# Recurrence pairs moved between attention's pairs in the first pass, memory pairs moved to its end, and the second query block of a head requested with the first

## The chip, the cores and the metric

The kernel runs on one core of a Trainium2 chip. Five engines work side by side: TensorE (PE in the profile, its weight loads PEld), VectorE (DVE), ScalarE (ACT), GpSimd (POOL) and SyncE (SP), which here issues nearly all DMAs. The metric is the device time of one execution in microseconds; the median of three runs of the kernel before is 1471.98 us (1469.74 to 1475.14).

## What is computed

One decoder layer for one sequence of 2048 tokens of width 1024, in float32. The input is normalised, projected once, and the projection's columns feed three groups of heads; their outputs are joined, projected again, normalised and added to the input.

```
hn = rms_norm(x, g_pre);  proj = hn @ w_in                      # 2048 x 4096
rg_x, rg_g, da_q, da_k, da_v, da_g, xa_q, xa_g = split(proj)    # 512 columns each
# recurrence group ("rg")
xc = causal_depthwise_conv(rg_x, conv_w, conv_b)                # width 4
r, i = sigmoid(xc @ w_rg_a + b_a), sigmoid(xc @ w_rg_x + b_x)   # per 64-wide head
a = exp(-8 r softplus(-lru_lambda));  u = sqrt(1 - a*a) * (i * xc)
h[t] = a[t] h[t-1] + u[t];  y_rg = h * silu(rg_g)
# differential attention, 4 heads, causal ("qk", "v", "g")
p = softmax(q1 k1^T / 8) - lam * softmax(q2 k2^T / 8);  o = p @ v
y_da = rms_norm(o, g_subln) * (1 - lambda_init) * silu(da_g)
# memory cross attention, 4 heads, 256 memory tokens ("xa")
y_xa = softmax(xa_q km^T / sqrt(128)) @ vm * silu(xa_g)         # km, vm from rms_norm(mem) @ w_mem_kv
out = x + rms_norm(concat(y_rg, y_da, y_xa) @ w_out, g_post)
```

## The kernel before, in words

Every float32 product is made of three products of a high and a low part (`mm3`), so a projection unit of 128 columns by 512 tokens is 24 matmuls. The sequence is cut into four chunks of 512 tokens. `project` is called twice: the first pass takes chunks 0 and 1, the second chunks 2 and 3. Each pass walks through 16 positions; at each it takes one pair of column blocks from `PAIRS` (lines 41 to 48), in four units (u = 0 to 3: two chunks, two blocks). The list has, by index: 0 and 1, queries and keys of heads 0 and 1 ("qk"); 2 and 3, values and gates of those heads ("v", "g"); 4 and 5, queries and keys of heads 2 and 3; 6 and 7, their values and gates; 8 to 11, the memory group ("xa"); 12 to 15, the recurrence group ("rg"). The first pass takes them in this order (`range(16)`, line 944); the second has an order of its own, `ORDER_B` (line 50): 0, 12, 2, 13, 1, 14, 3, 15, 4, 8, 6, 9, 7, 10, 11, 5.

**Weights.** In the first pass `w_conv` splits each piece of weights into high and low part, on ScalarE and GpSimd, and loads the piece three further on (`w_load`); the split pieces are stored to the DRAM tiles `WD[pair][piece]` (line 341) and read back from there in the second pass (line 334). `wsrc` (line 316) lists the pieces in the order of use.

**The order of TensorE's work** is written out by the program. Side work lives in generators (`spawn`), and `pump` lets those go on whose planned time has come, after every three matmuls of the projection. A planned clock (`now`) counts matmuls alone. `drain` lets the side work go on without the projection until a condition holds. The order on the other engines is made by the framework's scheduler, from priorities (`tc.high_priority`) and its own estimates.

- *Attention* is two streams, started at position 2 by `start_attention` (line 909): `s_stream` (line 698) makes scores and softmax for jobs of 256 queries, with a planned distance of 3.08 us between score steps in the first pass, and `t_stream` (line 773) transposes the probabilities and multiplies them with the values. The first 16 jobs are the first 1024 queries of heads 0 to 3; `s_stream` may hold 12 buffers of probabilities. `t_stream` does not begin a head before that head's gate pair is stored (line 778), and the keys and values of head 3 are not loaded before the second pass (line 660).
- *Queries.* `q2_load(i)` (line 702) asks for query block i, two blocks a job, with two DMAs on SP's queue from the DRAM tile `QD`. Block 2j is asked for while the job before it runs (or, for the very first, as soon as its pair is stored, line 709); block 2j+1 when block 2j is taken up (line 721).
- *Memory group.* `ev_xa` (line 518) evicts a unit; `xa_steps` (line 532) makes scores, softmax and output. At its first unit (line 857) the pass drains until no recurrence work is alive, drops the recurrence weights (`rgh`) and loads the memory's keys and values (`load_km`, four DMAs of 512 KB).
- *Recurrence group.* `ev_rg` (line 583) evicts a unit and, for the first block, makes the convolution on VectorE (L597, L600, cast L603) and the low part of its result on GpSimd (L604); it drains memory work for odd chunks. `rg_gates` (line 614) waits until no memory work is alive, loads and splits the recurrence weights if they are not there (`rg_weights`, line 575), makes the two gates (matmul into `rgo`), and then the scan (L637) and the product with the gate (L640).
- *Next chunks.* At position 13, `next_x` (line 919) drains until the first 12 jobs (heads 0 to 2) are done, and starts the norms of chunks 2 and 3 (`norm_steps`, scaling at L291); at position 15 the transposes of chunk 2 begin.

Of the kernel before, what the change touches and what calls it, by code (L numbers as in the profile page):

```python
# [46 lines left out]
    + [("rg", b, (b, 4 + b)) for b in range(4)]  # L47
)

ORDER_B = (0, 12, 2, 13, 1, 14, 3, 15, 4, 8, 6, 9, 7, 10, 11, 5)  # L50
MEM_PAIRS = [(0, 1), (2, 3), (4, 5), (6, 7)]

# [5 lines left out]
def hybrid_layer(  # L58
# [30 lines left out]
    def f4(name, shape=(128, 1024), dt=F32, pool=p4):  # L89
        return pool.tile(list(shape), dt, tag="f4", name=name)  # L90

    def f2(name, shape=(128, 516), dt=F32, pool=p2):
        return pool.tile(list(shape), dt, tag="f2", name=name)
# [7 lines left out]
    def ps_s(name, shape=(128, 512)):  # L101
        return psS.tile(list(shape), F32, tag="S", name=name)
# [7 lines left out]
    def asf(ap):  # L110
        return ap.bitcast(F32)
# [7 lines left out]
    WD = [[dr.tile([128, 1024], F32, name=f"WD{p}{i}") for i in range(4)] for p in range(16)]  # L119
# [77 lines left out]
    def mm(o, w, xx, start, stop):  # L197
        nc.tensor.matmul(o, w, xx, start=start, stop=stop)  # L198
        now[0] += max(o.free_size(), 256) / 2400.0
# [8 lines left out]
    def store(fn, delay):  # L208

        def go():  # L210
            fn()
            return
            yield
        spawn(go(), delay)
# [22 lines left out]
    def split_weight(raw, hi, lo, eng=nc.gpsimd):  # L237
        nc.scalar.copy(hi, raw)  # L238
        eng.tensor_sub(lo, raw, asf(hi))  # L239
# [73 lines left out]
    def pair_pieces(ps):  # L313
        return [w_in[4 * p + i] for p in ps for i in range(4)]

    wsrc = (pair_pieces(range(2)) + [w_mem[i] for i in range(16)] + pair_pieces(range(2, 16))
            + pair_pieces(ORDER_B))
    MEM0, WB0 = 8, 80
    wraw, wcv = {}, {}

    def w_load(*ids):
        for i in ids:
            if i < WB0:
                wraw[i] = praw.tile([128, 512], F32, tag="raw", name="wraw")
                nc.sync.dma_start(wraw[i], wsrc[i])

    def w_conv(*ids, eng=nc.gpsimd, pool=pw):
        for i in ids:
            if i < len(wsrc) and i not in wcv:
                w = wcv[i] = f4("wp", (128, 2, 2, 256), F32R, pool)  # L330
                if i >= WB0:

                    q = ORDER_B[(i - WB0) // 4]
                    nc.sync.dma_start(asf(w).rearrange("p a b c -> p (a b c)"), WD[q][i % 4])
                    continue
                split_weight(wraw.pop(i), w[:, 0].rearrange("p a b -> p (a b)"),
                             w[:, 1].rearrange("p a b -> p (a b)"), eng)
                w_load(i + 3)
                if not MEM0 <= i < MEM0 + 16:
                    q = i if i < MEM0 else i - 16  # L340
                    store(lambda w=w, q=q: nc.sync.dma_start(
                        WD[q // 4][q % 4], asf(w).rearrange("p a b c -> p (a b c)")), 4.0)


    def load_rows(src, n, name):
# [18 lines left out]

    hnT = {}
    memT = []
    state = {}
    ready = set()
    stored = set()
    setup()  # L370
# [5 lines left out]
    for i in range(4):  # L376
        nc.sync.dma_start(xb[:, i].rearrange("p a b -> p (a b)"), x[CH + i * 128:CH + (i + 1) * 128, :])
    mrows = load_rows(mem, 2, "memx")
    w_conv(0)
    for row in xr0:  # L380
        norm_row(row)
    w_conv(1, 2, eng=nc.vector)

    def woven(c, rows):
# [266 lines left out]
    def has(kind, idx, part):  # L651
        return (kind, idx, part) in stored
# [35 lines left out]
    def load_q2(h, qb):  # L688
        t = f2("q2", (128, 2, 2, 128), F32R)
        cs = slice((qb % 4) * 128, (qb % 4) * 128 + 128)  # L690
        for ab in range(2):
            nc.sync.dma_start(asf(t[:, ab]), QD[h][qb // 4][:, ab:ab + 2, :, cs].rearrange("c l r t -> (l r) c t"))
        return t

    def pace(i):
        return PACE[0 if "b" not in state else 2 if state["kind"] == "out" else 1][i]

    def s_stream(jobs):

        q2s = {}  # L700

        def q2_load(i):
            if i < 2 * len(jobs) and i not in q2s:
                h, pr = jobs[i // 2]
                if has("qk", h, pr // 4):
                    q2s[i] = load_q2(h, 2 * pr + i % 2)
        due = now[0]
        for ij, (h, pr) in enumerate(jobs):
            while 2 * ij not in q2s:
                q2_load(2 * ij)  # L710
                yield 0.5
            while kready.get((h, pr // 4), 1e9) > now[0]:
                yield 0.5
            due = max(due, now[0] - 3.0)
            ks = kt[h, pr // 4]
            P = []
            for b in range(2):
                qb = 2 * pr + b
                q2_load(2 * ij + b)
                q2 = q2s.pop(2 * ij + b)  # L720
                q2_load(2 * ij + b + 1)
                kend = (qb + 1) * 128
                nk = (kend + 511) // 512
                nm = tiny.tile([128, 2, nk], F32, tag="nm", name="nm")
                l = tiny.tile([128, 2, nk], F32, tag="l", name="l")
                e = {}
                for kc in range(nk):
                    w = min(512, kend - 512 * kc)
                    while room["e"] < 2:
                        yield 0.4  # L730
                    room["e"] -= 2
                    for c in range(2):
                        e[kc, c] = f2("e", (128, 512), pool=pe)
                        s = ps_s("s")
                        for ab in range(2):
                            mm(s[:, 0:w], q2[:, ab, c, :], ks[kc][:, c, 0:w], ab == 0, ab == 1)
                        with tc.high_priority(offset=PRS):
                            if kc == nk - 1:
                                nc.vector.tensor_add(s[:, w - 128:w], s[:, w - 128:w], cmask)
                            nc.vector.tensor_reduce(out=nm[:, c, kc:kc + 1], in_=s[:, 0:w], op=ALU.max, axis=AX.X,  # L740
                                                    negate=True)
                            nc.scalar.activation(e[kc, c][:, 0:w], s[:, 0:w], AF.Exp, bias=nm[:, c, kc:kc + 1],  # L742
                                                 accum_out=l[:, c, kc:kc + 1])
                        due += pace(0)
                        yield max(S_GAP, due - now[0])
                with tc.high_priority(offset=PRN):
                    f = tiny.tile([128, 2, nk], F32, tag="f", name="f")
                    if nk == 1:
                        nc.vector.reciprocal(f, l)
                        nc.vector.tensor_mul(f[:, 1, :], f[:, 1, :], nlam)  # L750
                    else:
                        m = tiny.tile([128, 2, 1], F32, tag="m", name="m")
                        r = tiny.tile([128, 2, 1], F32, tag="r", name="r")
                        nc.vector.tensor_reduce(out=m, in_=nm, op=ALU.min, axis=AX.X)
                        nc.vector.tensor_sub(f, m.to_broadcast([128, 2, nk]), nm)
                        nc.scalar.activation(f, f, AF.Exp)
                        nc.vector.tensor_mul(l, l, f)
                        nc.vector.tensor_reduce(out=r, in_=l, op=ALU.add, axis=AX.X)
                        nc.vector.reciprocal(r, r)
                        nc.vector.tensor_mul(r[:, 1, :], r[:, 1, :], nlam)  # L760
                        nc.vector.tensor_mul(f, f, r.to_broadcast([128, 2, nk]))  # L761
                    for kc in range(nk):
                        w = min(512, kend - 512 * kc)
                        e1, e2 = (e[kc, c][:, 0:w] for c in range(2))
                        nc.gpsimd.tensor_scalar(e2, e2, f[:, 1, kc:kc + 1], 1.0, op0=ALU.mult, op1=ALU.mult)  # L765
                        nc.vector.scalar_tensor_tensor(e1, e1, f[:, 0, kc:kc + 1], e2, op0=ALU.mult, op1=ALU.add)  # L766
                P.append([e[kc, 0] for kc in range(nk)])
                room["e"] += nk
            probs[h, pr] = now[0] + pace(1), P
            if pr == 7:  # L770
                room["kv"] += 1
# [167 lines left out]
    def start_b():  # L939
# [1 line left out]
        room["kv"] += 1  # L941
        spawn(prep_next(3))

    project((0, 1), 0, range(16), {
        (2, 0): start_attention,
        (13, 0): next_x,
        (15, 2): lambda: spawn(prep_next(2)),
# [30 lines left out]

    project((2, 3), 80, ORDER_B, {(0, 0): start_b, (15, 2): last_pair})

# [117 lines left out]
```

## Time and profile before

| | us |
|---|---|
| median of three runs | 1471.98 |
| the three runs | 1469.74, 1471.98, 1475.14 |
| the profiled execution, as timed | 1467.53 |
| its span, from the first to the last instruction | 1465.7 |
| TensorE busy | 1412.3 |
| VectorE busy | 898.3 |
| ScalarE busy | 775.9 |
| GpSimd busy | 477.3 |

The share of a busy engine is taken over the whole span. Matmul durations overlap, so TensorE's busy time is the union of them. By the eviction instructions, the first pass's positions 4 to 11 run from 153 to 425 us of the span (memory pairs from 275 on), its positions 12 to 15 (recurrence) from 425 to 548, the second pass's positions 0 to 7 from 548 to about 787, its memory pairs between 800 and 1080; from 1080 on the output projection runs. The clock in the tables is the mean granted to TensorE, 1.00 being full speed.

### The profile page before, as it was taken

To read this page: it belongs to the slowest core of one execution; us is meant where nothing else is said; L and a number is where in the kernel's file an instruction comes from. 1 tells how busy PE (TensorE), PEld (TensorE's weight loads), DVE (VectorE), ACT (ScalarE), POOL (GpSimd) and SP (SyncE) were. 2 spreads that over 40 slices of the span, in tenths; PEclk is the share of its full clock that TensorE was granted. 3 is DMA by queue.
4 is the path that set the end of the run, shared out by engine and by line. 5 is a ranking of instruction groups with operands and counts; after the bars stand their busy time and mean duration, and the time that the engine had idled before them with its cause. 6 is when DMAs were issued, how large, how long until landed. Compare 5 with 4: busy or idle time off the path is not lost.

```text
span 1465.7 us, 21854 instructions
## 1 busy us (share of the span) xinstructions
PE 1412.3 (96%) x7568; PEld 1199.2 (82%) x7568; DVE 898.3 (61%) x1872; ACT 775.9 (53%) x1900; POOL 477.3 (33%) x568
## 2 busy tenths in 40 slices
PE   5999999999999899999999999999999999999997
PEld 3798889888887678888887898888877888888886
DVE  6531555676644876746547666757678777767222
ACT  6343544666547784745555545555566545554221
POOL 2031333344435632412213222212255333334221
PEclk9999999999999999999999999999999999999999
DMA  8689787745433348356324554232475334322231
GB/s 298 180 263 338 230 240 237 247 143 181 166 119 110 134 163 247 121 173 196 114 97 118 165 177 168 86 113 70 143 251 169 101 135 150 102 76 94 87 122 72
DMA packets 147870, 234.37 MB, mean 160 GB/s; under 512 B 12464, under 2 KB 82224, under 8 KB 147760
## 3 DMA queue, kind: packets, MB, share of 16 engines
q1 hardware_dynamic: 147616, 232.98, 48.8%
q8 instruction: 59, 0.97, 0.3%
q14 instruction: 51, 0.42, 0.1%
q10 hardware_dynamic: 144, 0.01, 0.0%
HBM read 142.76 MB, written 90.18 MB: 159 GB/s over the span
## 4 chain that ended last, share of the span: by engine, by line
PE 73%; DVE 9%; ACT 7%; DMA 4%; POOL 3%; issue 3%; SPq 1%; DVEq 0%; POOLq 0%; ACTq 0%
PE ip L198 36%; PE po L198 16%; PE s L198 7%; PE o L198 6%; PE pt L202 3%; PE xas L198 2%; DVE e L766 1%; DVE nm L740 1%; PE xao L198 1%; DMA q<-QD 1%; DVE xc L600 1%; PE rgo L198 1%; ACT e L742 1%; PE xat L202 1%; POOL e L765 1%
## 5 line engine op out<-in xcount | busy, mean ns | idle before, releaser
L198 PE MATMUL ip<-hnT,wp 128*128 128x512 f32 x2688 | 680.5, 397 | 6.9 <-DVE rgg L610 2.6
L198 PEld LDWEIGHTS ip<-hnT,wp 128*128 128x128 f32 x2688 | 496.0, 190 | 109.8 <-DVE hnT L307 4.5
L742 ACT ACTIVATE e<-s,nm 128x512 f32<-128x512 f32 (+3 forms) x320 | 200.1, 626 | 254.7 <-DVE nm L740 235.8
L740 DVE TENSOR_REDUCE nm<-s 128x1 f32<-128x512 f32 (+3 forms) x320 | 193.4, 605 | 37.4 <-PE s L198 33.1
L198 PE MATMUL po<-wout,yg 128*128 128x512 f32 x768 | 193.4, 393 | 5.0 <-POOL wout L239 2.4
L765 POOL TENSOR_SCALAR e<-e,f 128x512 f32<-128x512 f32 (+3 forms) x160 | 121.3, 773 | 235.5 <-DVE f L761 161.6
L198 PE MATMUL s<-kv,q 128*128 128x512 f32 (+3 forms) x640 | 182.9, 367 | 3.9 <-DMA q<-QD 2.4
L198 PEld LDWEIGHTS po<-wout,yg 128*128 128x128 f32 x768 | 141.1, 188 | 35.4 <-POOL wout L239 4.2
L766 DVE SCALAR_TENSOR_TENSOR e<-e,f 128x512 f32<-128x512 f32 (+3 forms) x160 | 138.0, 887 | 29.9 <-POOL e L765 29.7
L807 DVE TENSOR_TENSOR pthl<-pt,pthl 128x512 fp32r<-128x512 f32 (+1 forms) x144 | 94.5, 656 | 68.0 <-ACT pthl L806 67.5
L198 PE MATMUL o<-pthl,kv 128*128 128x256 f32 (+1 forms) x864 | 134.3, 290 | 1.0 <-DVE pthl L807 0.9
L198 PEld LDWEIGHTS s<-kv,q 128*128 128x128 f32 x640 | 114.5, 189 | 25.1 <-DMA q<-QD 3.0
L239 POOL TENSOR_TENSOR wp<-wraw,wp 128x512 fp32r<-128x512 f32 x67 | 91.1, 1368 | 127.1 <-ACT wp L238 110.8
L198 PEld LDWEIGHTS o<-pthl,kv 128*128 128x128 f32 x864 | 114.1, 189 | 4.5 <-DVE pthl L807 1.8
L806 ACT CAST pthl<-pt 128x512 fp32r<-128x512 f32 (+1 forms) x144 | 80.7, 561 | 55.2 <-PE pt L202 54.5
L239 POOL TENSOR_TENSOR yg<-yraw,yg 128x512 fp32r<-128x512 f32 x48 | 64.2, 1341 | 132.8 <-ACT yg L238 122.4
L198 PE MATMUL ip<-wp,hnT 128*128 128x256 f32 x768 | 99.7, 284 | 1.3 <-POOL wp L239 0.8
L198 PEld LDWEIGHTS ip<-wp,hnT 128*128 128x128 f32 x768 | 95.8, 191 | 3.0 <-POOL wp L239 1.0
L198 PE MATMUL po<-wo,yg 128*128 128x512 f32 x384 | 97.2, 392 | 0.0
L202 PE MATMUL pt<-ident,e 128*128 128x128 f32 x544 | 83.0, 272 | 3.3 <-DVE pthl L807 3.3
L198 PEld LDWEIGHTS po<-wo,yg 128*128 128x128 f32 x384 | 71.0, 188 | 14.3
L202 PEld LDWEIGHTS pt<-ident,e 128*128 128x128 f32 x544 | 66.9, 140 | 18.4 <-DVE pthl L807 3.8
(188 smaller groups left out, 1686.1 us busy)
## 6 DMA issues: line engine op xcount, KB each, us to landing
WD<-wp SPq DMA_DIRECT2D x64, 512.0 KB, 4.7
wp<-WD SPq DMA_DIRECT2D x64, 512.0 KB, 4.3
wraw<-in_w_in_dram SPq DMA_DIRECT2D x64, 256.0 KB, 3.4
q<-QD SPq DMA_DIRECT2D x128, 128.0 KB, 3.7
kv<-KD SPq DMA_DIRECT2D x24, 512.0 KB, 5.9
kv<-VD SPq DMA_DIRECT2D x24, 512.0 KB, 6.2
yraw<-YD SPq DMA_DIRECT2D x48, 256.0 KB, 2.7
QD<-qkhl SPq DMA_DIRECT2D x32, 256.0 KB, 3.5
```

Of the source, the lines that this page charges most:

```text
L198: nc.tensor.matmul(o, w, xx, start=start, stop=stop)
L202: nc.tensor.transpose(o, i, ident)
L239: eng.tensor_sub(lo, raw, asf(hi))
L600: nc.vector.scalar_tensor_tensor(xc[:, 0:CH], xr[:, k:k + CH], vec2[:, cw + k:cw + k + 1], xc[:, 0:CH], op0=ALU.mult, op1=ALU.add)
L740: nc.vector.tensor_reduce(out=nm[:, c, kc:kc + 1], in_=s[:, 0:w], op=ALU.max, axis=AX.X, negate=True)
L742: nc.scalar.activation(e[kc, c][:, 0:w], s[:, 0:w], AF.Exp, bias=nm[:, c, kc:kc + 1], accum_out=l[:, c, kc:kc + 1])
L765: nc.gpsimd.tensor_scalar(e2, e2, f[:, 1, kc:kc + 1], 1.0, op0=ALU.mult, op1=ALU.mult)
L766: nc.vector.scalar_tensor_tensor(e1, e1, f[:, 0, kc:kc + 1], e2, op0=ALU.mult, op1=ALU.add)
L806: nc.scalar.copy(hi[:, 0:n], t[:, 0:n])
L807: nc.vector.tensor_sub(lo[:, 0:n], t[:, 0:n], asf(hi[:, 0:n]))
```

## The change

The first pass gets an order of its own, `ORDER_A`: the recurrence pairs (12 to 15) stand at positions 4, 6, 8 and 10, between the pairs 4, 6, 7 and 5 of attention's later heads, and the memory pairs (8 to 11) at positions 12 to 15. The list of weight pieces and the store index of the split pieces follow that order. `xa_live`, the count of memory work that is alive, starts at 0 in the state, since the recurrence now asks for it before any memory pair has run. When the first query block of a head's first job (the one with `pr == 0`) is asked for, the second is asked for in the same step.

```diff
+ORDER_A = (0, 1, 2, 3, 12, 4, 13, 6, 14, 7, 15, 5, 8, 9, 10, 11)
 ORDER_B = (0, 12, 2, 13, 1, 14, 3, 15, 4, 8, 6, 9, 7, 10, 11, 5)
...
-    wsrc = (pair_pieces(range(2)) + [w_mem[i] for i in range(16)] + pair_pieces(range(2, 16))
+    wsrc = (pair_pieces(range(2)) + [w_mem[i] for i in range(16)] + pair_pieces(ORDER_A[2:])
             + pair_pieces(ORDER_B))
...
                     store(lambda w=w, q=q: nc.sync.dma_start(
-                        WD[q // 4][q % 4], asf(w).rearrange("p a b c -> p (a b c)")), 4.0)
+                        WD[ORDER_A[q // 4]][q % 4], asf(w).rearrange("p a b c -> p (a b c)")), 4.0)
...
-    state = {}
+    state = {"xa_live": 0}
...
                 if has("qk", h, pr // 4):
                     q2s[i] = load_q2(h, 2 * pr + i % 2)
+                    if pr == 0 and i % 2 == 0:
+                        q2_load(i + 1)
...
-    project((0, 1), 0, range(16), {
+    project((0, 1), 0, ORDER_A, {
```

## Rows read from the trace of the kernel before

**Rows 1.** The page, part 1: busy time, share of the span, instructions of each engine.
```profile
PE 1412.3 (96%) x7568; PEld 1199.2 (82%) x7568; DVE 898.3 (61%) x1872; ACT 775.9 (53%) x1900; POOL 477.3 (33%) x568
```

**Rows 2.** Windows: length; busy us of PE, PEld, DVE, ACT, POOL; clock, DMA share, GB/s.
```profile
125.00:150.00 25.00, 22.58 (x98) 18.27 (x97) 5.32 (x14) 9.58 (x21) 6.12 (x6) 0.94 0.84 295
153.00:425.00 272.00, 268.44 (x1516) 232.53 (x1515) 170.27 (x391) 151.38 (x393) 105.33 (x134) 1.00 0.62 199
275.00:425.00 150.00, 146.87 (x813) 125.85 (x812) 97.87 (x224) 86.72 (x230) 59.26 (x81) 1.00 0.48 159
425.00:548.00 123.00, 115.32 (x513) 92.06 (x512) 80.91 (x103) 89.71 (x179) 57.67 (x71) 0.97 0.40 134
475.00:500.00 25.00, 22.19 (x87) 16.88 (x86) 21.00 (x30) 20.06 (x46) 15.01 (x23) 0.93 0.34 116
548.00:716.00 168.00, 166.65 (x890) 142.87 (x890) 110.72 (x228) 91.48 (x216) 48.53 (x61) 1.00 0.57 177
716.00:787.00 71.00, 67.02 (x326) 55.46 (x325) 36.72 (x61) 42.05 (x86) 17.49 (x20) 0.98 0.34 114
```

**Rows 3.** Groups by line, PE, 425 to 548: busy, mean ns; idle before, releasers.
```profile
L198 PE MATMUL ip<-hnT,wp 128*128 128x512 f32 x397 | 98.8, 402 | 2.7 <-DVE rgg L610 2.6
L198 PE MATMUL rgo<-xchl,rgh 128*128 128x512 f32 x32 | 12.3, 424 | 3.9 <-POOL xchl L604 3.0 <-DVE xchl L603 0.7
```

**Rows 4.** Groups by line, PE, 153 to 425.
```profile
L198 PE MATMUL s<-kv,q 128*128 128x512 f32 (+3 forms) x136 | 36.3, 348 | 0.0
...
L198 PE MATMUL xas<-kmh,xaq 128*128 128x256 f32 x64 | 12.4, 286 | 2.8 <-DVE xaq L528 2.8
```

**Rows 5.** Groups by line, PE, 548 to 800.
```profile
L198 PE MATMUL s<-kv,q 128*128 128x512 f32 (+3 forms) x120 | 33.8, 363 | 1.0 <-ACT e L742 1.0
```

**Rows 6.** Chain of waits in order of time: start us, us, what.
```profile
136.71 8.90 DMA q<-QD
```

**Rows 7.** Timeline, SP and PE: start us, us, instruction xcount [idle before <-releaser].
```profile
79.44 0.68 SPq L692 DMA_DIRECT2D q<-QD  x1
...
145.65 0.81 PE L198 MATMUL s<-kv,q 128*128 128x256 f32 x2 [2.38 <-DMA q<-QD]
```

**Rows 8.** Groups by line, PE, 800 to 1080, second pass's memory pairs.
```profile
L198 PE MATMUL s<-kv,q 128*128 128x512 f32 (+3 forms) x176 | 51.8, 375 | 0.5 <-ACT xap L549 0.5
...
L198 PE MATMUL xas<-kmh,xaq 128*128 128x256 f32 x64 | 12.2, 285 | 0.6 <-DVE xaq L528 0.6
```

**Rows 9.** Groups by line, DVE, 425 to 548.
```profile
L600 DVE SCALAR_TENSOR_TENSOR xc<-xr,vec,xc 128x512 f32<-128x512 f32 x24 | 24.7, 1027 | 0.7
...
L291 DVE TENSOR_SCALAR xrow<-xrow,rs 128x512 f32<-128x512 f32 x8 | 7.4, 989 | 0.9 <-POOL rs L256 0.9
```

**Rows 10.** Timeline, 438 to 444: the recurrence weights' low part and the first gate matmul.
```profile
438.80 2.40 POOL L239 TENSOR_TENSOR rgl<-rgraw,rgh 128x1024 fp32r<-128x1024 f32 x1 [4.35 <-ACT rgh L238]
...
443.83 0.39 PE L198 MATMUL rgo<-xchl,rgh 128*128 128x512 f32 x1
```

**Rows 11.** DMA issues: queue, xcount, KB each, median us from issue to landing.
```profile
rgraw<-in_w_rg_dram SPq DMA_DIRECT2D x1, 512.0 KB, 5.0
```

**Rows 12.** Timeline, ACT: a gate's last unit, head 2's outputs, position 13's first unit.
```profile
271.60 0.58 ACT L260 ACTIVATE gs<-ip 128x512 f32<-128x512 f32 x1
...
331.03 0.36 ACT L823 COPY oa<-o 128x256 f32<-128x256 f32 x1
...
406.92 0.37 ACT L823 COPY oa<-o 128x256 f32<-128x256 f32 x1
...
457.90 0.57 ACT L592 COPY xr<-ip 128x512 f32<-128x512 f32 x1
```

**Rows 13.** Groups by line, DVE, 548 to 800.
```profile
L600 DVE SCALAR_TENSOR_TENSOR xc<-xr,vec,xc 128x512 f32<-128x512 f32 x24 | 18.8, 784 | 0.4
```

**Rows 14.** Timeline, 772 to 778, second pass's fourth recurrence pair.
```profile
772.73 1.27 DVE L637 TENSOR_TENSOR_SCAN ri<-rga,carry,ri 128x512 f32<-128x512 f32 x1
...
776.43 0.68 DVE L807 TENSOR_TENSOR pthl<-pt,pthl 128x512 fp32r<-128x512 f32 x1
...
777.16 0.66 PE L202 MATMUL pt<-ident,e 128*128 128x128 f32 x4 [3.35 <-DVE pthl L807]
```

## The prediction

> **What bounds the kernel now.** I start with the busy shares: TensorE is busy 96% of the span, and no other engine comes near [rows 1]. A change that keeps every matmul can win only what TensorE idles, plus what it loses while its clock is granted at half. Over the kernel it idles 1465.7 - 1412.3 = 53.4 us. The profiled execution took 1467.53 us, 4.45 us under the median of the runs, 1471.98; I make the sum against the first and carry the difference over to the second.
>
> Next come the stretches [rows 2]. Read in each TensorE's busy time against its length, and the granted clock. Positions 4 to 11 of the first pass run from 153 to 425 us: 272 us with 268.4 busy, so 3.6 idle, 3.1 of it in the four memory pairs (275 to 425). The four recurrence pairs that end the pass, 425 to 548, are different: 115.3 busy of 123, so 7.7 idle, at a clock of 0.97. The clock has two levels, 1.2 and 2.4 GHz; 0.97 over 123 us is worth 3.7 us of full-speed time, and it falls where TensorE had just waited (475 to 500: 2.8 idle, 0.93). So this stage loses 11.4 us. Nothing of attention runs there: 397 matmuls are projections, and TensorE waits for the gate product, for the split of the convolved input on GpSimd and for VectorE's cast before it [rows 3]. ScalarE (89.7 of 123) and VectorE (80.9) are crowded [rows 2], since the norms of the next chunks fall here too.
>
> The second pass already has the order that the change brings to the first, recurrence pairs alternating with attention's. There 548 to 716 idles 1.4 us, and 716 to 787 idles 4.0 us at 0.98, worth 1.4 more [rows 2]. It is a fair model: 136 score matmuls in 272 us of the first pass [rows 4] against 120 in 252 us [rows 5].
>
> Last, one DMA wait. The first head's second query block is requested at 136.71, takes 8.90 us to land [rows 6], and holds TensorE for 2.38 us at 145.65 [rows 7]; the clock of 125 to 150 is 0.94, another 1.5 us [rows 2]. Together 3.9 us.
>
> **The change, part by part.** No matmul is added or removed, and the weight pieces change only their order, each with its store index. So I count lost time.
>
> *Queries.* The second block of a head's first job is asked for with the first. For the first head that is right behind the request at 79.44 [rows 7], 57 us earlier, so the 8.90 us are covered: -3.9. On SP's queue its two issues pass ahead of the memory weights' load; those weights are loaded three pieces ahead, so I take nothing, and twice the 0.68 us of the issue at 79.44 if that cover is gone. One buffer is held 57 us longer, at a time when only norms share its pool. For the other heads the request moves by one block, and no other query wait is left on TensorE: 0.
>
> *Recurrence pairs leave the end of the pass*: -11.4. *Memory pairs leave positions 8 to 11*: -3.1.
>
> *Memory pairs last.* The trace has no memory pairs without attention and with the norms. Bounds: 1.1 us, the waits of the second pass's memory stretch (0.6 and 0.5) [rows 8], and the whole 11.4 of the present stage. These pairs need more of TensorE and less of the crowded engines than the recurrence, so I stay near the lower end: 3.1 as today, where the wait for the split queries (2.8) is the largest [rows 4], plus a stall behind the norms. VectorE scales eight row halves in one go of 7.4 us [rows 9], and the 25 us around it idle 2.8 [rows 2]. Sum +5.9.
>
> *Recurrence pairs between attention's.* +6.7, what 548 to 787 loses (1.4 + 4.0 + 1.4, rounded). Bounds: 1.4, the smooth part's idle time alone, and that plus several stalls, priced in rival 3.
>
> *Recurrence weights.* The memory pairs drop them, so the second pass loads them again: one DMA, a ScalarE cast and a GpSimd subtraction of 2.40 us, which ends at 441.2. The first gate matmul starts at 443.83 [rows 10], so 2.6 us of cover are left. The load lands in 5.0 us [rows 11]. The first of the two now falls into a busier stretch (DMA share 0.62 against 0.40 [rows 2]); the query load that took 8.90 us [rows 6] is the nearest row for a late one, 3.9 later and so 1.3 beyond the cover. I take +0.5 for both, between 0 and 2.6.
>
> *Moved, taken at nothing.* The hook at position 13 drains until three heads are done. Their last output is read at 406.92, and the first unit of position 13 is evicted at 457.90 [rows 12]: some 45 us of cover. The third head's gate pair goes from position 7 to 9, two positions of 34 us (272/8) later, so from 271.60 to about 340, against that head's first output at 331.03 [rows 12]. Its first output comes some 15 us late while its scores run ahead in the 12 buffers, and the outputs catch up before 407. If that cover goes, TensorE runs dry in the drain. The other drain, before the memory pairs, finds the last recurrence pair a whole pair behind. The memory keys and values are loaded once a pass, as now.
>
> Sum: -3.9 - 11.4 - 3.1 + 5.9 + 6.7 + 0.5 = **-5.3 us**. 1467.5 becomes 1462.2, and the median 1472.0 becomes 1466.7. That is -0.36%, inside the 0.5% (7.4 us) that a measurement of this kernel can tell from no change.
>
> **A rule weighed.** The convolution step on VectorE takes 1027 ns in the old last stage [rows 9] and 784 in the second pass [rows 13]. GpSimd is 47% busy in the first (57.7 of 123) and 28% in the second (66.0 of 239), and 39% in positions 4 to 11 (105.3 of 272) before the recurrence joins [rows 2]. The Trainium skill, GPSIMD Engine Reference, section Specifications, says that GpSimd shares its SBUF interfaces with VectorE and that instructions with two SBUF inputs contend for them. The trace agrees in direction.
>
> **Rivals.**
> 1. *GpSimd slows VectorE.* The pass's 24 convolution steps run at 1027 ns beside attention too, since the weight splits, which the second pass lacks, stay on GpSimd. That is 24 x 0.243 = 5.8 us of VectorE time more than my model stretch shows. If all lies on the path, the sum is +0.5: 1472.5. For it: the two durations. Against: VectorE is 63% busy in positions 4 to 11 (170.3 of 272) and can absorb some.
> 2. *Full gain.* The memory pairs lose 1.1, the recurrence 1.4: -3.9 - 11.4 - 3.1 + 1.1 + 1.4 + 0.1 = -15.8, giving 1456.2. For it: memory needs less of the crowded engines. Against: 716 to 787.
> 3. *VectorE's queue holds attention up: slower.* At 772.73 a recurrence scan, and then convolution steps, stand ahead of the probability split; the split starts at 776.43, and TensorE's transposes wait 3.35 us for it [rows 14]. With 1.4 of clock such an event costs 4.8. My forecast holds one in four pairs. One more leaves no change; three more (half of the eight chunks) make -5.3 + 14.3 = +9.0: 1481. For it: all four pairs meet attention. Against: first-pass jobs have one or two key pieces instead of three.
> 4. *The request does not move the wait.* The early load is held by its buffer or SP's queue: -5.3 + 3.9 = -1.4, giving 1470.6.
>
> **How the numbers follow.** Forecast 0.43, with its own range 1461 to 1473; full gain 0.25; VectorE's queue 0.15; GpSimd 0.10; request unmoved 0.07. The range 1456 to 1481 reaches to the full gain and to three extra stalls; half of each of these two cases, 0.2 in all, lies outside. Faster by over 0.5% is under 1464.6: the full gain and a quarter of the forecast, 0.36. Slower by over 0.5% is the third rival, 0.15. The rest, 0.49, is within.
>
> **What would show it.** Right: no query wait near 145 us and no half clock there; the first pass's last four pairs idle under 7 us; positions 4 to 11 idle 5 to 8; a second load of the recurrence weights early in the second pass, with no wait behind it. Wrong: transposes that wait for the probability split among the first pass's recurrence pairs (rival 3), convolution steps near 1 us there with gate matmuls waiting (rival 1), a hole before position 13 (the drain), or a last stage that idles as before, for then the norms set its loss and not the recurrence.

## The result, and the profile after

The changed kernel took 1489.62 us, the median of four runs (1488.08 to 1494.60), against 1470.86 for the kernel before beside it: a ratio of 1.013 with a 95% interval of 1.0096 to 1.0165. It is slower, by 19 us, where the forecast was 5 us faster, and the time lies above the range. The profiled execution of the changed kernel took 1489.34 us with a span of 1487.6 us; that is 21.9 us more than the profiled one before (1465.7).

The page's first part of the changed kernel says that the work is the same, and that TensorE's busy time has grown:

```profile
PE 1421.8 (96%) x7568; PEld 1205.8 (81%) x7568; DVE 890.4 (60%) x1872; ACT 776.1 (52%) x1901; POOL 477.2 (32%) x569
```

7568 matmuls as before [rows 1], but 9.5 us more of busy time, which points at matmuls that ran slower, and 1487.6 - 1421.8 = 65.8 us idle against 53.4. The windows of the changed kernel (columns as in [rows 2]) show where:

```profile
125.00:150.00 25.00, 25.00 (x117) 20.80 (x116) 7.63 (x20) 12.43 (x28) 9.03 (x10) 1.00 0.93 320
153.00:425.00 272.00, 252.64 (x1309) 214.10 (x1309) 187.53 (x379) 167.07 (x388) 126.69 (x144) 0.96 0.56 179
425.00:575.00 150.00, 142.11 (x732) 118.42 (x731) 62.83 (x126) 75.16 (x190) 36.86 (x62) 0.99 0.48 158
575.00:800.00 225.00, 220.25 (x1140) 186.16 (x1139) 134.78 (x264) 122.81 (x273) 61.80 (x76) 1.00 0.49 155
```

From 125 to 150 the query wait is gone: 25.00 busy of 25, clock 1.00, where [rows 2] has 22.58 at 0.94. From 153 to 425, though, where the kernel before idles 3.6 us at full clock, TensorE now idles 19.4 us, and the clock is 0.96. In the trace's clock records that stretch has four periods at half clock, of 3.41 us once and 6.83 us three times; half of 23.9 us is 12 us more. So this stretch loses 31 us. VectorE is busy 188 of the 272 us and GpSimd 127: no engine but TensorE is near its limit on average.

To close the account I took, for each matmul, the time to the next matmul's start, less the lower quartile of that time for its form. Summed, this "lost time" holds waits and slow clock together:

| stretch, us | before | after | change | forecast |
|---|---|---|---|---|
| 0 to 100 | 16.8 | 18.2 | +1.4 | 0 |
| 100 to 150 (query wait) | 6.6 | 0.5 | -6.1 | -3.9 |
| 150 to 425 (positions 4 to 11) | 17.3 | 44.0 | +26.7 | -3.1 + 6.7 |
| 425 to 575 (end of the pass) | 15.5 | 14.5 | -1.0 | -11.4 + 5.9 |
| 575 to the end | 59.9 | 60.4 | +0.5 | +0.5 |

The changes add up to +21.5 of the 21.9 us. One row makes the result.

### The profile page after: what moved, and what is told of

Read it like the earlier page. It is cut to its first block, busy times and chain, and to the rows that moved or that the text cites. A ratio compares the mean times of both kernels' runs of the same rounds, so it can differ in the third digit from the quotient of the medians.

```text
span 1487.6 us, 21843 instructions
## 1 busy us (share of the span) xinstructions
PE 1421.8 (96%) x7568; PEld 1205.8 (81%) x7568; DVE 890.4 (60%) x1872; ACT 776.1 (52%) x1901; POOL 477.2 (32%) x569
## 5 line engine op out<-in xcount | busy, mean ns | idle before, releaser
L744 DVE TENSOR_REDUCE nm<-s 128x1 f32<-128x512 f32 (+3 forms) x320 | 192.8, 604 | 36.1 <-PE s L200 32.5
L770 DVE SCALAR_TENSOR_TENSOR e<-e,f 128x512 f32<-128x512 f32 (+3 forms) x160 | 141.4, 907 | 37.3 <-POOL e L769 37.1
L200 PEld LDWEIGHTS po<-wo,yg 128*128 128x128 f32 x384 | 71.0, 188 | 14.3
```

## What TensorE waits for

The groups by line of the changed kernel, TensorE, 153 to 425, have two waits that are not in [rows 4]:

```profile
L200 PE MATMUL s<-kv,q 128*128 128x512 f32 (+3 forms) x132 | 36.5, 359 | 5.7 <-ACT e L746 5.7
L200 PE MATMUL o<-pthl,kv 128*128 128x256 f32 (+1 forms) x168 | 28.2, 298 | 12.3 <-DVE pthl L811 7.0 <-ACT pthl L810 5.1 <-DVE m L758 0.2
```

Scores wait until ScalarE has read the scores before them (`e`), and the products with the values wait for the split probabilities (`pthl`). Both are attention's own chain, not the recurrence's. There is one such stall for each recurrence pair, near 185, 250, 324 and 401 us, and each brings its period at half clock. The timeline of the changed kernel from 313 to 327 us, VectorE first, then GpSimd, ScalarE and TensorE, shows the third:

```profile
313.87 1.18 DVE L770 SCALAR_TENSOR_TENSOR e<-e,f 128x512 f32<-128x512 f32 x1 [0.59 <-POOL e L769]
314.97 1.67 DVE L599 TENSOR_SCALAR xc<-xr,vec 128x512 f32<-128x512 f32 x1
316.56 1.77 DVE L770 SCALAR_TENSOR_TENSOR e<-e,f 128x512 f32<-128x512 f32 x1
318.26 1.78 DVE L602 SCALAR_TENSOR_TENSOR xc<-xr,vec,xc 128x512 f32<-128x512 f32 x1
319.96 0.29 DVE L743 TENSOR_TENSOR s<-s,cmask 128x128 f32<-128x128 f32 x1
320.16 1.55 DVE L602 SCALAR_TENSOR_TENSOR xc<-xr,vec,xc 128x512 f32<-128x512 f32 x1
321.63 0.28 DVE L744 TENSOR_REDUCE nm<-s 128x1 f32<-128x128 f32 x1
...
323.49 1.18 DVE L754 TENSOR_TENSOR f<-f,nlam 128x1 f32<-128x1 f32 x1
...
315.06 2.72 POOL L241 TENSOR_TENSOR wp<-wraw,wp 128x512 fp32r<-128x512 f32 x2
317.75 1.74 POOL L638 TENSOR_TENSOR ri<-ri 128x512 f32<-128x512 f32 x1
319.45 1.71 POOL L241 TENSOR_TENSOR wp<-wraw,wp 128x512 fp32r<-128x512 f32 x1
323.38 1.27 POOL L606 TENSOR_TENSOR xchl<-xc,xchl 128x512 fp32r<-128x512 f32 x1 [2.22 <-DVE f L753]
...
321.94 0.37 ACT L746 ACTIVATE e<-s,nm 128x128 f32<-128x128 f32 x1 [5.70 <-DVE nm L744]
...
323.94 0.50 PE L200 MATMUL o<-pthl,kv 128*128 128x256 f32 x2 [3.44 <-ACT pthl L810]
```

Read it from the bottom. TensorE waits 3.44 us for the cast `pthl`; that cast stands behind `e` on ScalarE, which idles 5.70 us for the row maximum `nm`; and the row maximum stands on VectorE behind five instructions of 512 columns that take 1.2 to 1.8 us each. The same forms take much less elsewhere: L602 has 784 ns in the second pass of the kernel before [rows 13, its L600]. Work out the ends: the second L770 ends at 318.33, 0.55 us after the first two splits (317.78); the two L602 end at 320.04 and 321.71, 0.55 us after GpSimd's L638 (319.49) and after its third split (321.16). Each looks as if it began its own work when GpSimd's instruction ended. The clearest is L754, one element per partition, 1.18 us long, from 323.49 to 324.67: GpSimd's L606 runs from 323.38 to 324.65. The other L754 of the stretch agree. There are ten; five run beside a GpSimd instruction, take 0.32, 0.46, 0.57, 0.62 and 1.18 us, and each ends 0.01 to 0.02 us after the end of that instruction or of the one that it met first. The other five take 0.16 us.

That gave three theories. **A:** GpSimd's operations on SBUF hold VectorE's up while they run. **B:** VectorE simply has too much work in front of attention's. **C:** no contention, but in-order queues: VectorE waits for GpSimd's products, with attention's instructions behind it.

## The experiments

**The two parts by themselves.** First the early request alone, with the old order.

```diff
-ORDER_A = (0, 1, 2, 3, 12, 4, 13, 6, 14, 7, 15, 5, 8, 9, 10, 11)
+ORDER_A = tuple(range(16))
```

> The early query request alone, on the old order of the first pass. Both theories: the query wait of 2.4 us near 145 us and the half clock behind it are gone, the rest stays as in the kernel before: 3.9 us under it, about 1467. A second theory for this part, that the request only moves the wait (to the weights behind it on the DMA queue): 1471.

Measured: 1464.52 us (1463.87 to 1465.21) against 1470.9, ratio 0.9951 with an interval of 0.9934 to 0.9969. Its windows:

```profile
153.00:425.00 272.00, 268.40 (x1514) 232.32 (x1513) 167.34 (x387) 150.65 (x395) 104.30 (x135) 1.00 0.62 204
575.00:800.00 225.00, 219.22 (x1147) 186.50 (x1146) 140.65 (x268) 126.47 (x282) 65.82 (x77) 0.99 0.45 141
```

Then the order alone, without the early request.

```diff
-                    if pr == 0 and i % 2 == 0:
-                        q2_load(i + 1)
```

> The new order alone, without the early request. If the two parts add: the changed kernel plus 3.9, about 1493, with the query wait back near 145 us and the same idle stretches around 240, 310 and 390 us. If the early query loads themselves disturb the first recurrence pair (buffers, SP's queue): 1485 or less.

Measured: 1494.34 us, ratio 1.0156 (1.0134 to 1.0178). The request brings 6.4 us (4.6 to 9.7 by the interval) on the old order and 4.7 on the new; the order costs 25.1 with the request and 23.4 without. The parts add. From here on the kernel to stand beside is the early request alone, which loses 17.4 us from 150 to 425.

**GpSimd's weight splits taken away** for the pieces used from position 5 to 11.

```diff
-                split_weight(...)
+                if 36 <= i < 64:
+                    nc.scalar.copy(w[:, 0]..., wraw.pop(i))
+                    nc.sync.dma_start(asf(w)[:, 1]..., WD[0][i % 4][:, 512:1024])
+                else:
+                    split_weight(...)
```

> The changed kernel without GpSimd's subtraction for the weights of positions 5 to 11 of the first pass: their low parts are loaded by DMA from another pair's stored pieces instead, so this leaves that part of the split out and the values are not the layer's. Theory A (GpSimd's work beside attention stretches VectorE's instructions, and VectorE's queue then holds up attention): the small VectorE instructions return to 0.2 us and the convolution steps to 0.75, and the 31.7 us lost between 153 and 425 us (19.3 idle, 12.4 of clock) fall under 12: 1470 or less. Theory B (VectorE simply has too many instructions in front of attention's, whatever GpSimd does): at most a third goes, 1480 to 1490.

Measured: 1480.11 us, ratio 1.0058 (1.0037 to 1.0080).

```profile
153.00:425.00 272.00, 257.89 (x1356) 218.92 (x1355) 175.14 (x381) 170.68 (x395) 94.20 (x123) 0.97 0.68 215
```

GpSimd's busy time in the stretch falls by 32.5 us, and the kernel's time by 9.5. VectorE's busy time falls by 12.4 us although nothing was taken from it, and the stretch holds more matmuls (1356 against 1309); that speaks for A. But the gain is half of what A had promised, and the time lies at the lower edge of B's range (1480 to 1490), so the time alone did not decide. The run also has a wait of its own: scores wait 2.4 us for a query load, which in the changed kernel they do not; the extra loads for the low parts are the likely reason.

**VectorE's work taken away:** three of the convolution's four terms are left out in the first pass.

```diff
-            for k in range(1, 4):
+            for k in range(1, 4 if c > 1 else 1):
```

> The changed kernel with three of the four terms of the convolution left out in the first pass: 24 VectorE steps, about 25 us of its time, gone; GpSimd's work is whole. Theory B (too many VectorE instructions): the loss between 153 and 425 us falls from 31.7 under 12, 1470 or less. Theory A (GpSimd stretches what is there): the attention steps stay stretched and half of the loss or more stays, 1474 to 1486.

Measured: 1488.04 us, ratio 1.0112 (1.0090 to 1.0133). Its window:

```profile
153.00:425.00 272.00, 250.40 (x1332) 213.04 (x1331) 171.75 (x356) 168.13 (x391) 125.63 (x146) 0.98 0.57 182
```

VectorE is busy 171.75 us, about as in the kernel before (170.27, [rows 2]), and TensorE still idles 21.6. The time is 2 us above A's range too, and 18 above B's. B falls as the main cause: taking away 24 VectorE steps brings 1.6 us.

**The recurrence's three GpSimd operations moved to VectorE** in the first pass (all three lines alike).

```diff
-            nc.gpsimd.tensor_mul(i, i, r)
+            (nc.vector if c < 2 else nc.gpsimd).tensor_mul(i, i, r)
```

> The changed kernel, with the three wide GpSimd operations of a recurrence pair (low half of the convolved rows, input gate times rows, times the root) done by VectorE in the first pass. Theory A (a GpSimd operation on SBUF holds VectorE's SBUF operations up while it runs, and small ones in attention's chain pay most): some 33 us of GpSimd work leaves the stretch 153 to 425 while VectorE gets some 17 us more; 8 to 14 us of the loss go, 1476 to 1482. Theory B (VectorE has too much to do): over 1489.6. Theory C (no contention, but the recurrence's tail waits at the head of VectorE's in-order queue for GpSimd's products, which stand behind weight splits): the waits for GpSimd before the scan vanish and with them most of the loss, 1468 to 1478.

Measured: 1480.16 us, ratio 1.0055 (1.0035 to 1.0075), inside A's range and above C's. VectorE got more to do, and the kernel is 9.5 us faster than the changed one.

```profile
153.00:425.00 272.00, 257.75 (x1357) 219.10 (x1356) 196.35 (x405) 171.04 (x395) 102.99 (x125) 0.97 0.60 187
```

A and C could both claim that gain. **The next run parts them:** the same, but GpSimd does three products of the same size for which nobody waits (24 in all, 13.7 + 11.1 + 11.4 = 36 us in its trace).

```diff
+            if c < 2:
+                nc.gpsimd.tensor_mul(xr[:, 0:CH], xc[:, 0:CH], asf(xh[:, 0]))
...
+            if c < 2:
+                nc.gpsimd.tensor_mul(xc[:, 0:CH], xc[:, 0:CH], a)
...
+            if c < 2:
+                nc.gpsimd.tensor_mul(xc[:, 0:CH], xc[:, 0:CH], a)
```

> As the run before it (the three operations on VectorE), but GpSimd still does three products of the same size beside them, into rows that are no longer needed, and no instruction waits for their values. Theory A: the contention is back although nobody waits for GpSimd, so the gain of the run before is lost: 1488 or more. Theory C: as the run before, within 3 us.

Measured: 1496.44 us, ratio 1.0166 (1.0145 to 1.0187): 16 us over the run before it.

```profile
153.00:425.00 272.00, 247.28 (x1273) 208.37 (x1271) 204.92 (x400) 165.55 (x385) 130.58 (x143) 0.96 0.54 170
```

Work whose result nobody reads, on an engine that is busy 131 of 272 us, costs 16 us. The idle products can still hold up GpSimd's own queue, attention's scaling among them: VectorE waits 13.5 us for that scaling here, 10.4 in the run before. So the durations have to say whether VectorE is slowed. By form, VectorE, 153 to 425, in this kernel; both operands of the first row lie in SBUF, the second row's one input too:

```profile
L759 DVE TENSOR_TENSOR f<-f,nlam 128x1 f32<-128x1 f32 x10 | 4.8, 476 | 0.3
L763 DVE TENSOR_REDUCE m<-nm 128x2 f32<-128x4 f32 x12 | 1.8, 152 | 0.2
```

**Nearly all of that GpSimd work away:** the three operations on VectorE, and GpSimd's subtraction for the weights of positions 5 to 11 left out.

```diff
+                if 36 <= i < 64:
+                    rw = wraw.pop(i)
+                    nc.scalar.copy(w[:, 0]..., rw)
+                    nc.scalar.activation(w[:, 1]..., rw, AF.Copy, scale=2.0 ** -13)
```

> The three operations on VectorE, and GpSimd's subtraction for the weights of positions 5 to 11 left out as well (ScalarE writes a scaled copy of the weights into the low halves instead, so the products' values change): of GpSimd's work beside attention only attention's own scaling and the head's end are left. Theory A: VectorE's small operations run at 0.16 us again, granted clock 0.99 to 1.00 in 153 to 425, 1465 to 1472. Theory B: over 1489.6, since VectorE has more to do. Theory C: 1468 to 1478.

Measured: 1474.48 us, ratio 1.0013 (1.0001 to 1.0026): 15.1 us of the loss are gone (17 by the two ratios to the kernel before). That is 2.5 us over A's range and inside C's, so here too the durations decide. The window, and two products on VectorE with both operands in SBUF, of one element per partition and of four:

```profile
153.00:425.00 272.00, 261.44 (x1391) 222.85 (x1390) 182.66 (x408) 186.83 (x428) 66.00 (x100) 0.99 0.61 194
```

```profile
L758 DVE TENSOR_TENSOR f<-f,nlam 128x1 f32<-128x1 f32 x10 | 2.4, 237 | 0.3
L763 DVE TENSOR_TENSOR f<-m,nm 128x4 f32<-128x4 f32 x12 | 1.9, 160 | 0.3
```

In the changed kernel these are:

```profile
L759 DVE TENSOR_TENSOR f<-m,nm 128x4 f32<-128x4 f32 x12 | 4.6, 386 | 0.3
L754 DVE TENSOR_TENSOR f<-f,nlam 128x1 f32<-128x1 f32 x10 | 3.9, 394 | 0.3
L758 DVE TENSOR_REDUCE m<-nm 128x2 f32<-128x4 f32 x12 | 1.8, 152 | 0.2
```

So the mean of the one-element product is 394 ns with GpSimd's work as it was, 476 with the idle products and 237 with little GpSimd work (259 in the kernel before); the product of four elements falls from 386 to 160; and a reduction with one SBUF operand has 152 ns with the idle products as without. That GpSimd's operations hold VectorE's up, as A says, is shown. The Trainium skill, SBUF — State Buffer, section Who interferes with whom, says that VectorE and GpSimd share a pair of SBUF ports under an exclusive lock held for a whole instruction, and that instructions of VectorE with two SBUF inputs compete for it. The trace agrees: 1.18 us for L754, which ends with GpSimd's L606.

Is the holding up the whole of GpSimd's part? The rows speak against it. These are attention's combination `e` in the changed kernel, without the weight splits, and with the recurrence's operations on VectorE:

```profile
L770 DVE SCALAR_TENSOR_TENSOR e<-e,f 128x512 f32<-128x512 f32 (+3 forms) x34 | 31.9, 948 | 16.5 <-POOL e L769 16.5
L773 DVE SCALAR_TENSOR_TENSOR e<-e,f 128x512 f32<-128x512 f32 (+3 forms) x34 | 27.4, 816 | 17.0 <-POOL e L772 17.0
L769 DVE SCALAR_TENSOR_TENSOR e<-e,f 128x512 f32<-128x512 f32 (+3 forms) x34 | 29.2, 871 | 10.4 <-POOL e L768 10.4
```

Without the splits the instruction gets shorter (948 to 816 ns), but VectorE waits as long for GpSimd's scaling, 17.0 us. With the recurrence's operations on VectorE the wait falls to 10.4, near the 9.6 of the early request alone, and the scan's wait of 3.5 us goes, while the instruction is shorter by less (871). Each of the two runs gained 9.5 us. So waits in the in-order queues, of the kind that C names, are part of the loss beside the holding up; how the 15 us divide between them is not shown.

**What is left** after that run is 1474.5 - 1464.5 = 10 us, and the lost time puts it in the same stretch: 27.6 us from 150 to 425 against 17.4. The timeline of that kernel, 380 to 390 us, shows its largest stall:

```profile
381.90 1.54 DVE L610 TENSOR_TENSOR xchl<-xc,xchl 128x512 fp32r<-128x512 f32 x1
383.43 1.03 DVE L646 TENSOR_TENSOR ri<-ri,rgg 128x512 f32<-128x512 f32 x1
386.11 1.07 DVE L774 SCALAR_TENSOR_TENSOR e<-e,f 128x512 f32<-128x512 f32 x1 [0.83 <-POOL e L773]
388.81 0.69 ACT L750 ACTIVATE e<-s,nm 128x512 f32<-128x512 f32 x1 [2.62 <-DVE nm L748]
389.64 0.81 PE L199 MATMUL s<-kv,q 128*128 128x512 f32 x2 [3.67 <-ACT e L750]
```

Here two of the recurrence's instructions stand on VectorE ahead of attention's combination `e`, and the next row maximum behind that; VectorE also waits 0.83 us for attention's scaling on GpSimd. I tried whether that scaling is the rest, by moving it to ScalarE in the first pass.

```diff
+                        if "b" not in state:
+                            nc.scalar.activation(e2, e2, AF.Copy, scale=f[:, 1, kc:kc + 1])
+                        else:
                             nc.gpsimd.tensor_scalar(e2, e2, f[:, 1, kc:kc + 1], 1.0, ...)
```

> As the kernel without GpSimd's work for the recurrence and the weights of positions 5 to 11 (1474.5, still 10 over the early request alone), with attention's own scaling in the first pass moved from GpSimd to ScalarE as well (no value changes by that; the weights' low halves are still a scaled copy). If the rest of the loss is attention's scaling on GpSimd, for which VectorE waited 10.4 us in 153 to 425: 1466 to 1470, and the stall of TensorE behind ScalarE's e (4.5 us) goes. If it is the recurrence's six passes over ScalarE standing before attention's exponentials: 1474 to 1480, since ScalarE gets some 20 us more.

Measured: 1474.93 us, ratio 1.0028 (1.0013 to 1.0042): no gain, and inside the range given for a crowded ScalarE. TensorE's stall behind ScalarE's `e` halves, from 4.5 to 2.2 us in 153 to 425, but ScalarE is busy 200 us there instead of 187, so a gain and a new cost may cancel; the run does not show that the scaling plays no part. That the rest is queueing on VectorE and ScalarE is what the rows above show for one stall; no run took those instructions away, so it is argued and not shown.

**One recurrence pair instead of four** between attention's.

```diff
+ORDER_A = (0, 1, 2, 3, 12, 4, 5, 6, 7, 8, 9, 10, 11, 13, 14, 15)
```

> The changed kernel with only the first of the four recurrence pairs moved: it stands between attention's pairs, memory's pairs are back at positions 9 to 12 and three recurrence pairs end the pass. The early request stays, so the run to stand beside is the early request alone, 1464.5. Theory A with a price per pair: some 28 us in 153 to 425 over four pairs are 7 for one, less a quarter of the 11.4 that the pass's end loses to recurrence pairs: 1467 to 1471. If a stall comes only when recurrence pairs follow one another closely: 1462 to 1465.

Measured: 1473.34 us (1470.93 to 1477.52), ratio 1.0021 (1.0010 to 1.0032): 8.8 over the early request alone, above what either theory gave. The lost time says why both missed. From 150 to 425 one pair costs 3.9 us (21.3 against 17.4), less than a quarter of the four; but the end of the pass loses 4.3 more (20.9 against 16.6), where I had taken a quarter off. TensorE's group there, 425 to 548:

```profile
L199 PE MATMUL rgo<-xchl,rgh 128*128 128x512 f32 x23 | 9.8, 469 | 8.2 <-DVE xchl L604 5.9 <-POOL xchl L605 2.2
```

Three recurrence pairs wait 8.2 us at their gates where four waited 3.9 [rows 3], since VectorE's cast before them is late. What makes it late was not tried.

**Using it.** In the second pass recurrence pairs stand between attention's pairs in both kernels, so A should pay there too. The early request alone, with the three operations on VectorE in both passes:

> The early request alone (order of the kernel before), with the recurrence's three operations on VectorE in both passes. In the second pass these pairs stand between attention's pairs in the kernel before too. Theory A: contention goes there as well, 3 to 6 us under the early request alone: 1458 to 1462. Theory B: VectorE gets 34 us more work in all, 1466 to 1472. Theory C: 1460 to 1463.

Measured: 1461.06 us (1458.92 to 1464.95), ratio 0.9921 (0.9905 to 0.9938), inside the ranges of A and C alike. Then in the second pass only (`c > 1`), with the first as it was:

> The early request alone, with the recurrence's three operations on VectorE in the second pass only, where its pairs stand between attention's pairs, and on GpSimd in the first, where they end the pass. If the 3.5 us that VectorE in both passes gained came from the second pass (575 to 800 kept TensorE busy for 221.8 us instead of 219.2): 1459 to 1462, at or a little under it. If they came from the first pass's end: 1463 to 1465.

Measured: 1459.12 us (1458.87 to 1460.24), ratio 0.9927 (0.9913 to 0.9942). Its window of the second pass:

```profile
575.00:800.00 225.00, 221.91 (x1169) 189.21 (x1168) 148.95 (x295) 129.32 (x288) 35.69 (x53) 1.00 0.45 142
```

GpSimd is busy 30 us less than in the early request alone, VectorE 8 us more, and TensorE gains 2.7 us of work in the same 225 us, with the clock at 1.00. Whether A or C pays here is not parted: VectorE's scan in this window, in the early request alone and in this kernel, loses its wait for GpSimd and gets a little shorter as well.

```profile
L638 DVE TENSOR_TENSOR_SCAN ri<-rga,carry,ri 128x512 f32<-128x512 f32 x8 | 11.3, 1407 | 5.8 <-POOL ri L637 5.8
L638 DVE TENSOR_TENSOR_SCAN ri<-rga,carry,ri 128x512 f32<-128x512 f32 x8 | 10.7, 1343 | 0.1
```

And with attention's scaling of the second pass on ScalarE as well:

> As the run before it, with attention's scaling in the second pass on ScalarE instead of GpSimd too. Theory A: less GpSimd work beside VectorE's chain, 1457 to 1461. If ScalarE, whose exponentials and casts stand in the same chain, is crowded by some 20 us more: 1463 to 1470.

Measured: 1459.48 us, ratio 0.9937 (0.9918 to 0.9956), no more. The lowest median is that of the early request with the old order and the recurrence's three operations on VectorE in the second pass: 11 us under the kernel before, 30 under the changed one. The intervals of the last three kernels overlap (ratios 0.9921, 0.9927 and 0.9937), so they are not told apart.

## Why the prediction was wrong

**The step that failed** is "Recurrence pairs between attention's. +6.7", and in it the sentence that calls the second pass "a fair model". The stretch loses 31 us there (19.4 idle and 12 of clock), and by the lost time this stretch makes 23 of the 27 us between the forecast and the profile. I compared the two passes by how many score matmuls fall in them [rows 4, 5], which is TensorE's side. What differs is GpSimd: the first pass splits weights there, the second reads them back split. I had the numbers in hand (39% busy in positions 4 to 11 before the recurrence joins, 28% in the second pass with it, [rows 2]), and the changed kernel has 127 of 272, 47%. The runs show GpSimd's work beside attention as the cause of some 15 us of the 25 that the order costs; the other 10 stay open.

- *Rival 1, GpSimd slows VectorE*, had the right mechanism, but the wrong instructions and price. It counted 5.8 us of longer convolution steps; in the changed kernel these take 907 ns, less than I gave. What costs is in attention's chain, where stretched instructions and waits for GpSimd's queue delay a row maximum, an exponential and a cast in turn, until TensorE waits and its clock falls. I gave it a chance of 0.10. By the run with little GpSimd work its part is some 1489.6 - 1474.5 = 15 us.
- *Rival 3, VectorE's queue holds attention up*, had the right place and the right sign: the rows of the third stall are its scan, convolution and late split again. It allowed four stalls of 4.8 us each, one of them already in the forecast: 1481. There were four, one for each recurrence pair of the first pass, at 31 / 4 = 7.8 us each on average, and in three of them the clock stayed low for 6.83 us instead of 3.41. Its argument against itself, that first-pass jobs have fewer key pieces, did not hold.
- *Memory pairs last, +5.9, and the end of the pass, -11.4*: 425 to 575 came out 1.0 lower in all instead of 5.5, so with the -11.4 as it stands the memory pairs cost some 10.4 there and not 5.9. From 425 to 575 the changed kernel idles 7.9 us at a clock of 0.99. Its groups by line there show the waits, for the split queries as named, and for the probabilities' scaling on GpSimd, which I had not named:

```profile
L200 PE MATMUL xas<-kmh,xaq 128*128 128x256 f32 x64 | 12.0, 283 | 2.4 <-DVE xaq L530 2.4
L204 PE MATMUL xat<-ident,xap 128*128 128x128 f32 x64 | 10.3, 276 | 2.8 <-POOL xap L555 2.4
```

- *Queries, -3.9*: right in place, and a little low. The wait and the low clock at 146 us are gone, and the runs say 6.4 with an interval from 4.6.
- *Recurrence weights, +0.5*: right. The second load has its low part ready at 612.6 us and the first gate matmul runs at 615.42, in the changed kernel:

```profile
610.19 2.41 POOL L241 TENSOR_TENSOR rgl<-rgraw,rgh 128x1024 fp32r<-128x1024 f32 x1 [1.29 <-ACT rgh L240]
...
615.42 0.40 PE L200 MATMUL rgo<-xchl,rgh 128*128 128x512 f32 x1
```

- *Moved, taken at nothing* (the drain before position 13, the third head's gate pair): no wait of TensorE for them shows in the groups by line, and from 425 to 575 the waits above are the largest. The "some 15 us late" of the third head's first output is 9 by the prediction's own numbers (340 less 331); nothing else rests on it.

The prediction named four signs of being wrong. Waits for the probability split came, though the products with the values wait for it (12.3 us) and the transposes do not (0.0). Convolution steps came near 1 us (907 ns), but no gate matmul waits from 153 to 425. No hole came before position 13. And the last stage idles as before: 7.9 us from 425 to 575 against 7.7, with waits of the memory group, and not of the norms, as the largest. The two rivals were priced as if each came alone. Added, they give -5.3 + 5.8 + 14.3 = +14.8 and 1486.8, and with the 4.5 us of the memory pairs 1491; the measured time lies between.

## What to carry to other kernels

Before work is moved beside a latency-bound chain, count for each engine pair what shares a resource there, not only whether each engine has room, and who waits in whose queue: here 24 products on GpSimd, 36 us in all, cost 16 us although nobody read them. A stage that is used as a model must match in the engines off the critical path too, and where a trace shows the same instruction at 0.16 and at 1.2 us, that row prices the interference. When two rivals feed the same wait, price them together.

## What I had not expected of the hardware

How long a very small instruction can be: 1.18 us for one element per partition (L754) beside a GpSimd operation, against 160 ns for a like one of four elements without (L763 in the kernel with little GpSimd work). The recurrence's scan, whose two inputs both lie in SBUF, seems at first to escape: its means in 153 to 425 are 1284 and 1208 ns in the changed kernel, 1282 and 1216 in the kernel with little GpSimd work. But it meets the same interference. In the kernel before, one scan is held behind a GpSimd split that began 0.07 us earlier, and takes 2.30 us:

```profile
492.89 1.29 POOL L604 TENSOR_TENSOR xchl<-xc,xchl 128x512 fp32r<-128x512 f32 x1
492.96 2.30 DVE L637 TENSOR_TENSOR_SCAN ri<-rga,ri 128x512 f32<-128x512 f32 x1 [1.45 <-POOL ri L636]
```

The split ends at 494.18 and the scan at 495.26, 1.08 us later. Where the scan begins first, GpSimd's instruction is the long one: in the changed kernel a scan runs from 683.28 to 684.55, and L606, which starts at 683.44, takes 2.20 us where its median is 1.30. And in the kernel that leaves out three terms of the convolution, four scans from 153 to 425 have a mean of 1748 ns, in the stretch where the changed kernel's had 1208.

Instructions that read scores from PSUM kept their time: the mask L743 took 0.29 us at 319.96, in the middle of GpSimd's third split, between two neighbours of 1.78 and 1.55 us.
